# Hybrid attention layer on one core: scalings on ScalarE ordered behind the newest weight cast

## The chip, the core and the metric

The kernel runs on one core of a Trainium2 chip. The metric is the time of one execution on the device, in microseconds (us), median of the runs shown. Five engines work side by side, each through its own queue in order: TensorE (PE in the profile; its weight loads are PEld), VectorE (DVE), ScalarE (ACT), GpSimd (POOL) and SyncE (SP), which here only issues DMAs.

## The reference

One decoder layer over 256 tokens of width 2048, all in float32:

```python
mod = jax.nn.silu(c) @ w_ada + b_ada
shift, scale, gate = jnp.split(mod, 3, axis=-1)
h = _rms_norm(x, g_norm) * (1.0 + scale[:, None, :]) + shift[:, None, :]
proj = h @ w_in
qa, ka, va, za, q_idx, k_idx, w_idx, qb, kb, vb, zb = jnp.split(proj, COL_SPLITS, axis=-1)
qa = _rms_norm(qa.reshape(heads_a), q_norm_a)      # ka, qb, kb alike; k_idx over its 64 columns
ya = _dsa_attention(qa, ka, va, q_idx, k_idx, w_idx, _alibi_slopes(N_HEADS_A))
yb = _moba_attention(qb, kb, vb, _alibi_slopes(N_HEADS_B))
ya = ya.reshape(B, L, D_A) * jax.nn.silu(za)       # yb alike
y = jnp.concatenate([ya, yb], axis=-1) @ w_out
return x + gate[:, None, :] * y
```

`w_in` is 2048 by 9296, `w_out` 2048 by 2048, `w_ada` 2048 by 6144. Group a has eight heads of 128 columns that attend to 64 keys chosen by an indexer: sixteen small heads of 64 columns (`q_idx`), one shared key (`k_idx`), a relu, and a weighted sum give a score, and the 64 best keys stay. Group b has eight heads with plain causal attention, since 256 tokens are one block. What the change touches is the RMS norm of the queries, the keys and the indexer's key: each row of a head is multiplied by one over the root of its mean square.

## The kernel before

**Products.** Every weight is split in two parts before it is multiplied. ScalarE makes the high part (`cast_hi`, line 326, tile `wh`), VectorE the rest (`cast_lo`, line 336, tile `wl`), and TensorE makes three products of each block (lines 778 to 780: high by high, high by low, low by high). The unit is a step j: two blocks of 128 rows of weights by 512 columns, which is one cast `wh<j>`, one `wl<j>` and twelve matmuls (two blocks, two halves of the tokens, three products). `wh` and `wl` have four buffers each, and the weights as they land (`raw`) four of 8 KB a partition; SyncE issues a load as soon as a buffer of `raw` comes free. The casts are written two steps ahead of the matmuls (`LA = 2`, line 746).

**Order of the groups.** The columns of `w_in` are worked through in groups: the indexer's `i2`, `i0`, `i1`, then four quads of four heads, `b0`, `b1`, `a0`, `a1`, each as z, q, k, v; then the output product `mm_y`. A step's name in the profile says its group (`mm_h_vb` is a step of v of group b).

**Work between the steps.** Attention and norms are generators that `bg_q.step` advances after every step (line 788). Three of them matter here.
- `prep` (lines 504 to 518), for q and for k of each quad, as soon as its group is done: eight squares with sums on ScalarE (line 510), an add and a power -0.5 on GpSimd (`rsqrt`, lines 153 and 154), and eight scalings of 128 by 128 in place on ScalarE (line 517). The scalings need the power's result. `idx_k` does the same for the indexer's key with four scalings (line 456).
- `idx_pair` (lines 465 to 485), eight times, two index heads each: transposes `ptq` on TensorE (line 470), a copy `qi` out of PSUM on ScalarE (line 472), four small products `lg` on TensorE (lines 478 and 479), a relu `rl` for each head on ScalarE (line 481), and four additions on VectorE (line 483).
- `head` (lines 528 to 581): transposes of q and k, scores, exponentials, transposes (`pt`) and their copy `pT` on ScalarE (line 560), product with v (`pv`).

**What sets the order.** A scheduler builds one queue for each engine out of these written steps, and each engine takes its queue strictly from the front. An instruction that is not yet allowed to run holds up what is queued behind it on that engine. The helper `tc.add_manual_dep(..., NO_WAIT, ...)` (used by `in_order`, line 89) tells the scheduler that one instruction has to stand behind another of its engine; it adds no wait for a semaphore.

Of the kernel before, what the change touches and what calls it, by code (L numbers as in the profile page):

```python
# [10 lines left out]
AF = mybir.ActivationFunctionType  # L11
ALU = mybir.AluOpType

P = 128
# [4 lines left out]
HD = 128  # L19
# [29 lines left out]
NO_WAIT = mybir.DependencyInfo(mybir.DependencyClass.NoSync, mybir.DependencyReason.DATA)  # L49
# [3 lines left out]
def hybrid_block(ctx: ExitStack, tc: tile.TileContext, x, cols, w_ada_t, w_in, w_out, out):  # L53
    nc = tc.nc
# [11 lines left out]
    def late_tiles():  # L66
        if not late_pool:
            early.close()
            late_pool.append(ctx.enter_context(tc.tile_pool(name="late", bufs=2)))
        return late_pool[0]  # L70
# [12 lines left out]
    def ps_tile(tag, name):  # L83
        return psum.tile([P, 512], F32, tag=tag, bufs=1, name=name)

    last_on = {}

    @contextmanager
    def in_order():
# [61 lines left out]
    def rsqrt(dst, ssq, n):  # L151

        nc.gpsimd.tensor_scalar(dst, ssq, 1.0 / n, EPS, op0=ALU.mult, op1=ALU.add)
        nc.gpsimd.tensor_tensor(dst, dst, mhalf[:, :dst.shape[1]], op=ALU.pow)
# [46 lines left out]
    while turn:  # L201
# [22 lines left out]
        for k in range(seg0, end, 4):  # L224
            n = min(4, end - k)
# [76 lines left out]
    for li, ld in enumerate(loads):  # L302
        for m in ld.get("members", [ld] if ld["kind"] == "w" else []):
            n = len(m["kts"])
# [6 lines left out]
    def cast_hi(j):  # L311
        nonlocal next_load
        if j >= len(subs):
            return
        sb = subs[j]
        while next_load <= sb["li"]:
            issue(next_load + 6)
            if loads[next_load]["kind"] == "ada":
                gemv_todo.append(loads[next_load])
            next_load += 1  # L320
        flush_gemv()
        ld = sb["ld"]
        v = ld["v"][:, sb["o"]:sb["e"], :]
        n, w = v.shape[1], v.shape[2]
        hi = wsp.tile([P, 2, 512], F32R, tag="wh", name=f"wh{j}")
        nc.scalar.activation(hi[:, :n, :w], v, AF.Copy)  # L326
        sb["hi"] = hi

    def cast_lo(j):
# [11 lines left out]
    def flush_gemv():  # L341
        while gemv_todo:
            gemv(gemv_todo.pop(0))
# [94 lines left out]
    proj = {}  # L438
# [4 lines left out]
    sm = consts.tile([P, 64], F32, name="sm")  # L443

    def idx_k():
        for t in range(2):
            src = proj["i2", t]
            junk = work.tile([P, P], F32, name=f"junki{t}", tag="junk")
            nc.scalar.activation(junk[:, :64], src[:, 256:320], AF.Square, accum_out=sm[:, t:t + 1])
            nc.vector.tensor_scalar(w2[:, 16 * t:16 * t + 16], src[:, 320:336], 2.0 ** -5, None, op0=ALU.mult)  # L450
        rsqrt(sm[:, 2:4], sm[:, 0:2], 64)
        yield 0
        kk = late_tiles().tile([P, 384], F32, name="kk", tag="at", bufs=4)
        for t in range(2):
            for j in range(2):
                nc.scalar.activation(kk[:, t * P + j * 64:t * P + j * 64 + 64], proj["i2", t][:, 256:320],
                                     AF.Copy, scale=sm[:, 2 + t:3 + t])
        yield 0
        pt = ps_tile("pt", "ptk")
        for t in range(2):  # L460
            nc.tensor.transpose(pt[:, t * P:(t + 1) * P], kk[:, t * P:(t + 1) * P], ident)
        nc.scalar.activation(kiT, pt[:, :L], AF.Copy, scale=kidx_col)
        yield 0
# [40 lines left out]
    def prep(q, c):  # L504

        ssq = quad.setdefault((q, c), work.tile([P, 16], F32, name=f"ss{c}{q}", tag="ss", bufs=3))
        for t in range(2):
            for h in range(4):
                junk = work.tile([P, P], F32, name=f"j{c}{q}{t}{h}", tag="junk")
                nc.scalar.activation(junk, proj[c + q, t][:, h * HD:(h + 1) * HD], AF.Square,  # L510
                                     accum_out=ssq[:, 4 * t + h:4 * t + h + 1])
        rsqrt(ssq[:, 8:16], ssq[:, 0:8], HD)
        yield 2
        for t in range(2):
            for h in range(4):
                s = proj[c + q, t][:, h * HD:(h + 1) * HD]
                nc.scalar.activation(s, s, AF.Copy, scale=ssq[:, 8 + 4 * t + h:9 + 4 * t + h])
        yield 0

    def prep_z(q):  # L520
# [129 lines left out]
    with in_order():  # L650
        cast_hi(0)
        cast_lo(0)
        x_keep(0)
        start_mod()
        x_transpose(1)
# [5 lines left out]
    with in_order():  # L661
        for j in range(1, LA):
            cast_hi(j)
            cast_lo(j)
        x_keep(1)
# [45 lines left out]
    def group_done(g):  # L711

        if g[0] == "i":
            bg_q.done.add(g)
        if g == "i2":
            bg_q.add(chain(idx_k(), *[idx_pair(p) for p in (6, 7, 0, 1, 2, 3, 4, 5)], idx_top()), "top")
        if g[0] in "qk" and g[1] in "ab":
            bg_q.add(prep(g[1:], g[0]), "prep" + g)
        if g[0] == "k" and g[1] in "ab":
            pend.extend((g[1:], h) for h in range(4))  # L720
        if g[0] == "v":
            bg_q.done.add(g)
        if g[0] == "z":
            bg_q.add(prep_z(g[1:]), "prepz" + g[1:])

    total = len(subs)
    for j in range(total):
# [12 lines left out]
        if ld["kset"] == "y" and "xload" not in started:  # L740
            started.add("xload")
            for n in range(4):
                for t in range(2):
                    xr[n, t] = u_tile(f"xr{n}{t}")
                    nc.scalar.dma_start(xr[n, t], x[t * P:(t + 1) * P, n * 512:(n + 1) * 512])
        cast_hi(j + LA)
        cast_lo(j + LA)
        for c in ada_done:
# [73 lines left out]
```

## Time and profile before

| | us |
|---|---|
| median of 3 runs | 576.06 |
| lowest and highest run | 575.78, 577.69 |
| the profiled execution, its time | 576.41 |
| the profiled execution, its span on the core | 574.6 |
| PE busy | 553.2 (96%) |
| DVE busy | 443.5 (77%) |
| ACT busy | 319.5 (56%) |

The profile's times count from the span's start; the profiled execution's own time is 1.81 us more than its span. A page has the engines' busy time, the chain of work that ended last followed back from the last instruction, and the groups of instructions that cost most. Queries of the trace give instructions in order of time, with the idle time ahead of one and who ended it in brackets, and tables of busy time by stretch.

### The profile page before, as it was taken

What the parts mean: (1) busy time and instruction counts of PE and PEld (TensorE: products, weight loads), DVE (VectorE), ACT (ScalarE), POOL (GpSimd) and SP (SyncE); (2) the same over time, 40 slices, a digit from 0 to 9 for tenths busy, and PEclk for the clock granted to TensorE, in tenths of its full rate; (3) what the DMA queues carried; (4) which work ended last, traced back from release to release, by engine and by line L of the source; (5) the groups of instructions that cost most, each with busy time, mean ns of one, the idle gap of its engine ahead of it and who ended that gap; (6) DMA issues with size and microseconds to landing.
All of it is one profiled execution on the core that took longest, in us unless ns stands there. A gap on an engine that the chain in (4) does not pass through costs nothing.

```text
span 574.6 us, 7426 instructions
## 1 busy us (share of the span) xinstructions
PE 553.2 (96%) x2658; PEld 462.7 (81%) x2658; DVE 443.5 (77%) x681; ACT 319.5 (56%) x652; POOL 31.8 (6%) x56
## 2 busy tenths in 40 slices
PE   3889999999999999999899999999999999999996
PEld 2768888888889998887578888888888888887885
DVE  4887779898899888898789988697676575558452
ACT  4588564443444453577644577555775784554340
POOL 4100000000000000102100010200210110000000
PEclk9999999999999999999999999999999999999999
DMA  8999998997898988785864467787565458444701
GB/s 293 411 351 370 347 346 328 336 357 279 315 360 314 369 325 305 231 337 212 300 235 168 153 251 261 254 327 250 192 227 173 165 203 294 172 141 182 236 37 38
DMA packets 59670, 150.09 MB, mean 261 GB/s; under 512 B 3056, under 2 KB 9456, under 8 KB 53616
## 3 DMA queue, kind: packets, MB, share of 16 engines
q1 hardware_dynamic: 58480, 147.51, 71.0%
q10 hardware_dynamic: 1152, 2.10, 1.2%
q8 instruction: 21, 0.34, 0.2%
q14 instruction: 17, 0.14, 0.1%
HBM read 147.50 MB, written 2.10 MB: 260 GB/s over the span
## 4 chain that ended last, share of the span: by engine, by line
PE 88%; ACT 3%; DMA 2%; issue 2%; DVE 2%; POOL 2%; SPq 0%; DVEq 0%; ACTq 0%
PE mm_y_o L780 5%; PE mm_y_o L778 5%; PE mm_y_o L779 5%; PE mm_h_zb L778 3%; PE mm_h_zb L779 3%; PE mm_h_zb L780 3%; PE mm_h_i L780 3%; PE mm_h_i L779 3%; PE mm_h_i L778 3%; PE mm_h_qb L778 3%; PE mm_h_qb L779 3%; PE mm_h_qb L780 3%; PE mm_h_ka L779 3%; PE mm_h_qa L778 2%; PE mm_h_za L780 2%; PE mm_h_va L778 2%
## 5 line engine op out<-in xcount | busy, mean ns | idle before, releaser
L326 ACT ACTIVATE wh<-raw 128x1024 fp32r<-128x1024 f32 (+3 forms) x192 | 188.4, 991 | 148.0 <-PE mm_y_o L780 31.9
L336 DVE TENSOR_TENSOR wl<-raw,wh 128x1024 fp32r<-128x1024 f32 (+3 forms) x192 | 215.2, 1139 | 68.1 <-ACT wh L326 67.6
L293 DVE CUSTOM_DVE_ANT_0 raw<-raw,s_row 128x2048 f32<-128x2048 f32 (+1 forms) x49 | 110.0, 2245 | 4.9 <-DMA raw<-in_w_ada_t 4.8
L778 PE MATMUL mm_y_o<-wh,yT 128*128 128x512 f32 x128 | 51.6, 403 | 0.0
L779 PE MATMUL mm_y_o<-wl,yT 128*128 128x512 f32 x128 | 50.0, 391 | 0.0
L780 PE MATMUL mm_y_o<-wh,yT 128*128 128x512 f32 x128 | 49.9, 391 | 0.0
L778 PE MATMUL mm_h_i<-wh,hhi 128*128 128x384 f32 (+1 forms) x96 | 31.7, 330 | 0.0
L779 PE MATMUL mm_h_i<-wl,hhi 128*128 128x384 f32 (+1 forms) x96 | 31.5, 328 | 0.0
L780 PE MATMUL mm_h_i<-wh,hlo 128*128 128x384 f32 (+1 forms) x96 | 31.4, 328 | 0.0
L780 PEld LDWEIGHTS mm_y_o<-wh,yT 128*128 128x128 f32 x128 | 24.0, 188 | 5.2 <-DVE yT L579 0.2
L778 PEld LDWEIGHTS mm_y_o<-wh,yT 128*128 128x128 f32 x128 | 24.1, 188 | 4.7 <-ACT yT L578 0.2
L779 PEld LDWEIGHTS mm_y_o<-wl,yT 128*128 128x128 f32 x128 | 24.1, 188 | 4.6
L778 PE MATMUL mm_h_qa<-wh,hhi 128*128 128x512 f32 x64 | 25.7, 410 | 0.9 <-ACT wh L326 0.9
L778 PE MATMUL mm_h_zb<-wh,hhi 128*128 128x512 f32 x64 | 26.5, 413 | 0.0
L778 PE MATMUL mm_h_vb<-wh,hhi 128*128 128x512 f32 x64 | 26.1, 408 | 0.0
L779 PE MATMUL mm_h_za<-wl,hhi 128*128 128x512 f32 x64 | 25.1, 392 | 0.9 <-DVE wl L336 0.9
L778 PE MATMUL mm_h_kb<-wh,hhi 128*128 128x512 f32 x64 | 25.9, 407 | 0.0
L778 PE MATMUL mm_h_qb<-wh,hhi 128*128 128x512 f32 x64 | 25.6, 403 | 0.0
L779 PE MATMUL mm_h_zb<-wl,hhi 128*128 128x512 f32 x64 | 25.5, 398 | 0.0
L778 PE MATMUL mm_h_ka<-wh,hhi 128*128 128x512 f32 x64 | 25.5, 403 | 0.0
L778 PE MATMUL mm_h_va<-wh,hhi 128*128 128x512 f32 x64 | 25.4, 397 | 0.0
L780 PE MATMUL mm_h_zb<-wh,hlo 128*128 128x512 f32 x64 | 25.3, 398 | 0.0
(215 smaller groups left out, 1193.5 us busy)
## 6 DMA issues: line engine op xcount, KB each, us to landing
raw<-in_w_in SPq DMA_DIRECT2D x51, 1024.0 KB, 5.7
raw<-in_w_ada_t SPq DMA_DIRECT2D x47, 1024.0 KB, 6.3
raw<-in_w_out SPq DMA_DIRECT2D x16, 1024.0 KB, 5.3
raw<-in_w_in SPq DMA_DIRECT2D x17, 512.0 KB, 5.0
raw<-in_w_in SPq DMA_DIRECT2D x11, 768.0 KB, 5.3
x<-in_x SPq DMA_DIRECT2D x8, 256.0 KB, 7.3
xr<-in_x ACTq DMA_DIRECT2D x8, 256.0 KB, 8.4
raw<-in_w_in SPq DMA_DIRECT2D x3, 672.0 KB, 7.5
```

The costliest lines, as they stand in the source:

```text
L293: nc.vector.tensor_tensor_reduce(out=ld["v"], in0=ld["v"], in1=s_row[:, h0:h1], scale=1.0, scalar=0.0, op0=ALU.mult, op1=ALU.add, accum_ou ...
L326: nc.scalar.activation(hi[:, :n, :w], v, AF.Copy)
L336: nc.vector.tensor_tensor(lo[:, :n, :w], v, sb["hi"][:, :n, :w].bitcast(F32), op=ALU.subtract)
L778: nc.tensor.matmul(ps, a_hi, sb["hi"][:, i, :w], start=st, stop=False)
L779: nc.tensor.matmul(ps, a_hi, sb["lo"][:, i, :w], start=False, stop=False)
L780: nc.tensor.matmul(ps, a_lo, sb["hi"][:, i, :w], start=False, stop=en)
```

## The change

All scalings of `prep` and `idx_k` are put behind the newest high cast that has been written so far. Line numbers grow by 11 to 14 with it.

```diff
+    newest_cast = []
+
+    @contextmanager
+    def behind_cast():
+        traced = nc.cur_bb.bb.instructions
+        n = len(traced)
+        yield
+        for ins in traced[n:]:
+            if ins.engine == newest_cast[-1].engine:
+                tc.add_manual_dep(ins, newest_cast[-1].name, NO_WAIT, reason="behind_cast")
...
         nc.scalar.activation(hi[:, :n, :w], v, AF.Copy)
+        newest_cast.append(nc.cur_bb.bb.instructions[-1])
...
-        for t in range(2):
-            for j in range(2):
-                nc.scalar.activation(kk[:, t * P + j * 64:t * P + j * 64 + 64], proj["i2", t][:, 256:320],
-                                     AF.Copy, scale=sm[:, 2 + t:3 + t])
+        with behind_cast():
+            for t in range(2):
+                for j in range(2):
+                    nc.scalar.activation(kk[:, t * P + j * 64:t * P + j * 64 + 64], proj["i2", t][:, 256:320],
+                                         AF.Copy, scale=sm[:, 2 + t:3 + t])
...
-        for t in range(2):
-            for h in range(4):
-                s = proj[c + q, t][:, h * HD:(h + 1) * HD]
-                nc.scalar.activation(s, s, AF.Copy, scale=ssq[:, 8 + 4 * t + h:9 + 4 * t + h])
+        with behind_cast():
+            for t in range(2):
+                for h in range(4):
+                    s = proj[c + q, t][:, h * HD:(h + 1) * HD]
+                    nc.scalar.activation(s, s, AF.Copy, scale=ssq[:, 8 + 4 * t + h:9 + 4 * t + h])
```

There are 68 such scalings (four for the indexer's key, eight for q and eight for k of each of four quads). In the built programs the queues of PE, DVE, POOL and SP are the same before and after, and so is ACT's but for three scalings at two places.

The first place is ACT's queue while PE is on v of quad b0. `p_kb0_0` and `p_kb0_1` are the keys of quad b0 for either half of the tokens, scaled in place by `sskb0`; `wh106` to `wh108` are casts of weights, `qi3`, `rl6` and `rl7` belong to pair 3 of the index heads. Before:

```order
L510 ACTIVATE jkb013_2541,sskb0_2526<-p_kb0_1_784 128x128
L517 ACTIVATE p_kb0_0_782<-p_kb0_0_782,sskb0_2526 128x128 x2
L326 ACTIVATE wh106_2606<-raw98_2399 128x1024
L472 ACTIVATE qi3_2568<-ptq3_2565 128x256
L517 ACTIVATE p_kb0_0_782<-p_kb0_0_782,sskb0_2526 128x128 x2
L517 ACTIVATE p_kb0_1_784<-p_kb0_1_784,sskb0_2526 128x128 x4
L326 ACTIVATE wh107_2635<-raw98_2399 128x1024
L481 ACTIVATE rl6_2589<-lg6_2586 128x384
L481 ACTIVATE rl7_2596<-lg7_2593 128x384
L326 ACTIVATE wh108_2667<-raw99_2460 128x1024
```

After, on the same engine:

```order
L523 ACTIVATE jkb013_2541,sskb0_2526<-p_kb0_1_784 128x128
L337 ACTIVATE wh106_2606<-raw98_2399 128x1024
L485 ACTIVATE qi3_2568<-ptq3_2565 128x256
L531 ACTIVATE p_kb0_0_782<-p_kb0_0_782,sskb0_2526 128x128 x4
L531 ACTIVATE p_kb0_1_784<-p_kb0_1_784,sskb0_2526 128x128 x4
L337 ACTIVATE wh107_2635<-raw98_2399 128x1024
L494 ACTIVATE rl6_2589<-lg6_2586 128x384
L494 ACTIVATE rl7_2596<-lg7_2593 128x384
L337 ACTIVATE wh108_2667<-raw99_2460 128x1024
```

Two scalings have moved from ahead of `wh106` and `qi3` to behind them, and all eight now stand in a row.

The second place is ACT's queue while PE is on k of quad a1. `p_qa1_0` and `p_qa1_1` are the queries of quad a1, `pTa01` is the transposed probabilities of head 1 of quad a0. Before:

```order
L326 ACTIVATE wh157_4176<-raw138_3963 128x1024
L517 ACTIVATE p_qa1_0_503<-p_qa1_0_503,ssqa1_4118 128x128
L326 ACTIVATE wh158_4201<-raw138_3963 128x1024
L560 ACTIVATE pTa01_4169<-pta01_4165 128x384
L517 ACTIVATE p_qa1_0_503<-p_qa1_0_503,ssqa1_4118 128x128 x3
L517 ACTIVATE p_qa1_1_505<-p_qa1_1_505,ssqa1_4118 128x128 x4
L326 ACTIVATE wh159_4267<-raw139_3965 128x1024
```

After:

```order
L337 ACTIVATE wh157_4176<-raw138_3963 128x1024
L337 ACTIVATE wh158_4201<-raw138_3963 128x1024
L574 ACTIVATE pTa01_4169<-pta01_4165 128x384
L531 ACTIVATE p_qa1_0_503<-p_qa1_0_503,ssqa1_4118 128x128 x4
L531 ACTIVATE p_qa1_1_505<-p_qa1_1_505,ssqa1_4118 128x128 x4
L337 ACTIVATE wh159_4267<-raw139_3965 128x1024
```

One scaling has moved from ahead of `wh158` and `pTa01` to behind them.

PE's queue, which is the same in both, has this at the first place (the twelve matmuls of a step are shown by their first and last; the names are those of the program before):

```order
L470 MATMUL ptq3_2565<-ident_81,p_i1_1_658 128x128
L778 MATMUL mm_h4_vb0_0_2551<-wh103_2494,hhi6_1058 128x512
...
L780 MATMUL mm_h4_vb0_1_2552<-wh103_2494,hlo7_1066 128x512
L478 MATMUL lg6_2586<-kiT_182,qi3_2568 128x128
L479 MATMUL lg6_2586<-kiT_182,qi3_2568 128x256
L478 MATMUL lg7_2593<-kiT_182,qi3_2568 128x128
L479 MATMUL lg7_2593<-kiT_182,qi3_2568 128x256
L778 MATMUL mm_h4_vb0_0_2551<-wh104_2547,hhi8_1315 128x512
```

Nothing has moved on PE: the four `lg` products of pair 3 stand between the step of `wh103` and the step of `wh104`, and they take `qi3`.

## Rows read from the trace of the kernel before

**Rows 1.** The page: busy time by engine; the chain's shares by engine.

```profile
PE 553.2 (96%) x2658; PEld 462.7 (81%) x2658; DVE 443.5 (77%) x681; ACT 319.5 (56%) x652; POOL 31.8 (6%) x56
...
PE 88%; ACT 3%; DMA 2%; issue 2%; DVE 2%; POOL 2%; SPq 0%; DVEq 0%; ACTq 0%
```

**Rows 2.** Stretches: us, then PE, PEld, DVE, ACT, POOL busy; PEclk, DMA share, GB/s.

```profile
282.60:285.20 2.60, 0.07 (x1) 0.00 (x0) 0.26 (x1) 1.93 (x5) 0.64 (x1) 0.97 0.86 328
285.30:288.50 3.20, 3.20 (x12) 2.26 (x13) 3.20 (x4) 3.20 (x9) 0.00 (x0) 0.51 0.01 4
298.00:567.00 269.00, 269.00 (x1298) 223.76 (x1297) 192.71 (x363) 156.45 (x366) 15.01 (x12) 1.00 0.58 201
```

**Rows 3.** Chain of waits in order of time, 280 to 287: start, us, what.

```profile
281.50 1.75 POOL sskb L154
...
284.91 0.28 ACT qi L472
...
285.23 0.81 PE lg L478 x4
```

**Rows 4.** Timeline of PE, 282 to 298: start, us, instruction, idle before it and its releaser.

```profile
282.29 0.39 PE L780 MATMUL mm_h_vb<-wh,hlo 128*128 128x512 f32 x1
285.23 0.81 PE L478 MATMUL lg<-kiT,qi 64*128 64x128 f32 x4 [2.56 <-ACT qi L472]
...
290.42 0.38 PE L470 MATMUL ptq<-ident,p_i 128*128 128x128 f32 x2
...
293.19 0.39 PE L780 MATMUL mm_h_vb<-wh,hlo 128*128 128x512 f32 x1
293.50 0.50 PE L478 MATMUL lg<-kiT,qi 64*128 64x128 f32 x4
...
297.23 0.38 PE L470 MATMUL ptq<-ident,p_i 128*128 128x128 f32 x2
```

**Rows 5.** Timeline of ACT, 283 to 291, same columns.

```profile
283.27 0.69 ACT L517 ACTIVATE p_kb<-p_kb,sskb 128x128 f32<-128x128 f32 x2 [2.19 <-POOL sskb L154]
283.87 1.04 ACT L326 ACTIVATE wh<-raw 128x1024 fp32r<-128x1024 f32 x1
284.82 0.36 ACT L472 ACTIVATE qi<-ptq 128x256 f32<-128x256 f32 x1
285.08 1.85 ACT L517 ACTIVATE p_kb<-p_kb,sskb 128x128 f32<-128x128 f32 x6
286.84 1.04 ACT L326 ACTIVATE wh<-raw 128x1024 fp32r<-128x1024 f32 x1
287.79 0.84 ACT L481 ACTIVATE rl<-lg 128x384 f32<-128x384 f32 x2
290.62 1.06 ACT L326 ACTIVATE wh<-raw 128x1024 fp32r<-128x1024 f32 x1 [1.99 <-PE mm_h_vb L780]
```

**Rows 6.** Timeline of the DMA queue on SP, 268 to 283.

```profile
270.16 2.71 SPq L280 DMA_DIRECT2D raw<-in_w_in  x2
```

**Rows 7.** The page, DMA issues: count, KB each, median us from issue to landing.

```profile
raw<-in_w_in SPq DMA_DIRECT2D x51, 1024.0 KB, 5.7
```

**Rows 8.** Timeline of ACT, 454 to 457.

```profile
454.70 0.40 ACT L517 ACTIVATE p_qa<-p_qa,ssqa 128x128 f32<-128x128 f32 x1 [0.72 <-POOL ssqa L154]
455.01 1.04 ACT L326 ACTIVATE wh<-raw 128x1024 fp32r<-128x1024 f32 x1
455.95 0.47 ACT L560 ACTIVATE pTa<-pta 128x384 f32<-128x384 f32 x1
```

**Rows 9.** Timeline of PE, 460 to 461.

```profile
460.31 0.59 PE L567 MATMUL pva<-pTa,p_va 128*128 128x256 f32 x2
```

**Rows 10.** Timeline of POOL, 400 to 460.

```profile
405.61 3.74 POOL L154 TENSOR_TENSOR ssqa<-ssqa,mhalf 128x8 f32<-128x8 f32 x1
...
453.03 1.64 POOL L154 TENSOR_TENSOR ssqa<-ssqa,mhalf 128x8 f32<-128x8 f32 x1
```

**Rows 11.** Timeline of DVE at three places.

```profile
284.94 1.23 DVE L336 TENSOR_TENSOR wl<-raw,wh 128x1024 fp32r<-128x1024 f32 x1 [3.20 <-ACT wh L326]
...
405.56 2.29 DVE L293 CUSTOM_DVE_ANT_0 raw<-raw,s_row 128x2048 f32<-128x2048 f32 x1 [2.03 <-DMA raw<-in_w_ada_t]
...
454.01 1.23 DVE L336 TENSOR_TENSOR wl<-raw,wh 128x1024 fp32r<-128x1024 f32 x1 [1.18 <-ACT wh L326]
```

## The prediction

> **What bounds the kernel now.** Begin with the page: PE is busy 96% of the span, and 88% of the chain that ended last is PE's [rows 1]. So the question is not how much work ScalarE has (56%), but where PE stands still and whether the change is at such a place. The table by stretches then shows two things [rows 2]. From 298 to 567 PE is busy 269.00 of 269.00 us at a granted clock of 1.00 while the DMA engines are at 0.58: there is no wait on PE in which an earlier start could be lost. And between 282.60 and 285.20 PE is busy 0.07 of 2.60 us, followed by 3.2 us in which its clock is 0.51 of full speed. The chain of waits says what held PE there [rows 3]: GpSimd's power for the key norm (1.75 us), then ScalarE, whose `qi` copy releases the `lg` products. ScalarE's timeline gives the reason [rows 5]: it sat idle 2.19 us until the power was there, because two scalings of the keys stood at the front of its queue, and the cast `wh106` and the copy `qi3`, which need no power, stood behind them. PE's `lg` of pair 3 takes `qi3` and came at 285.23 after 2.56 us of idle time [rows 4].
>
> **The first place, step by step.** ScalarE was free at 283.27 - 2.19 = 281.08 [rows 5]. The two scalings now come later, so `wh106` can begin there, if its data and its buffer are there. The data (raw98) is the first of the pair of loads issued from 270.16 [rows 6]; at 5.7 us to landing [rows 7] it is there at about 276. Its buffer was last read by the step of `wh102`, which PE had behind it a whole step before 282.29. So both conditions are met with some 3 us to spare, estimated from these rows. The instruction behind the cast follows 284.82 - 283.87 = 0.95 us later, so `qi3` starts at 282.03 and, at 0.36 us, is done at 282.39. The hand-over to PE took 0.05 us before (284.82 + 0.36 = 285.18, `lg` at 285.23), which makes 282.44. PE itself can't be there before its last matmul of the step, at 282.29, and the usual 0.31 us to `lg` that the next round shows (293.19 to 293.50) [rows 4]: 282.60. So PE is now the later of the two, by 0.16 us, and the wait goes altogether.
>
> *Term 1, the wait*: 285.23 - 282.60 = 2.63 us.
>
> *Term 2, the clock*: from `lg` to the next `ptq` PE has four small products and twelve matmuls. In this round that took 290.42 - 285.23 = 5.19 us, in the next, the same work, 297.23 - 293.50 = 3.73 us [rows 4]. The difference is 1.46 us, and in just this stretch the granted clock was 0.51 (the 1.2 GHz level), against 1.00 (2.4 GHz) ahead of the wait and after it [rows 2]. The clock fell after PE had stood still, and nothing else in the stretch sets it apart. Without the wait I take the whole 1.46 back; the bounds are 0 and 1.46, and I take the upper one since the fall follows the idle time directly.
>
> **What the moved scalings delay.** They still start when the power is there, 283.27, as the squares that feed it have not moved. All eight now stand in a row: two took 0.60 (283.27 to 283.87), six 1.76 (285.08 to 286.84), so 2.36 us, and `wh107` starts at 285.63, which is 1.21 us earlier than before (286.84). With 0.95 for `wh107` and 0.84 for the two relus, `wh108` starts at 287.42 [rows 5]. Its buffer is free when the step of `wh104` ends, 282.60 + 3.73 = 286.33; its data, the second load of the pair (issued by 272.87), landed long before: between 285.30 and 288.50 the DMA engines were at 0.01, so what had been issued was all there [rows 2, 6]. `qi4` then starts at 288.37 and is done at 288.73. PE asks for it one round after `lg` of pair 3, that is at 282.60 + (293.50 - 285.23 - 1.46) = 289.41 [rows 4]. The margin is 289.41 - 288.73 - 0.05 = 0.63 us: small, but positive. From there ScalarE waits for PE to free a buffer, as it did before at 290.62 [rows 5], and the old pattern runs on, 4.09 us earlier. VectorE had been idle 3.20 us ahead of `wl106` [rows 11]; it gets that work earlier and has a step and more before PE needs it. The keys are used by transposes that stand after pair 4 on PE, so nobody waits for the scalings.
>
> **The second place.** ScalarE had 0.72 us of idle time ahead of the one scaling of qa1, and `wh158` and `pTa01` now start 1.03 us earlier (455.01 - 453.98) [rows 8]. The first to use `pTa01` is PE at 460.31 [rows 9], which is 460.31 - 456.42 = 3.89 us after the copy was done even before, and the step of `wh158` is later still. PE has no idle time there [rows 2]. The worth is 0; if I were wrong about that cover, at most the 1.03. The other 65 scalings stay where they were: they stood behind the newest cast already.
>
> **The sum.** 2.63 + 1.46 + 0 = 4.09 us less, against the profiled execution's 576.41: 572.32. That execution was 0.35 above the median, 576.06, so for the median I forecast 576.06 - 4.09 = 572.0 us, 0.71% less.
>
> **The rivals.**
>
> *The clock term does not come back.* If the slow stretch belongs to that point of the program and not to the wait, only term 1 is won: 576.06 - 2.63 = 573.4. Against it speaks that the clock is 1.00 all along until PE stands still. The Trainium skill, "TensorE: Matmul & The Clock Gate", section "What's actually happening", says that the clock's monitor runs free of the kernel, so that one and the same kernel shows slow stretches of different length from run to run. By that rule term 2 would lie between 0 and 1.46 by chance, and the time between 572.0 and 573.4. The three runs before speak for a steady one: without the slow stretch the profiled execution would have taken 576.41 - 1.46 = 574.95, and no run is below 575.78. Chance 0.07.
>
> *GpSimd's power comes later, and PE waits at pair 4 instead.* One power on GpSimd took 3.74 us, where a VectorE instruction (line 293) had begun 0.05 us ahead of it, and 1.64 us at 453.03, where VectorE's low cast began during the power, at 454.01, and neither was longer for it [rows 10, 11]. At the first place `wl106` now falls into the power's time: it can start at 282.1, the power starts at 281.50. That is the order of 453.03, so I take the power's time as it was. The Trainium skill, "SBUF — State Buffer", section "SBUF: two separate sides", says that GpSimd and a VectorE instruction with two inputs in SBUF lock each other out for a whole instruction, whoever began first. The slow power agrees with that; that the low cast at 454.01 kept its 1.23 us does not. Were the power as slow as the slowest row here (1.99 us more), the row of scalings would slip by as much, `qi4` would come 1.99 - 0.63 = 1.36 us late, and 2.73 us would be left: 573.3. Chance 0.05.
>
> *The gain is lost further on, or the change doesn't do what it says:* 576.1. What is won here could go into a later wait, if the next stretch were set by DMA or by VectorE. But from 298 on PE never waits [rows 2], and loads are issued when buffers come free, not at fixed times, so they move with PE. Or `wh106` finds its data or its buffer missing at 281.08, and `qi3` is as late as before. Only three of 68 instructions move, so without the first place there is nothing else to win. Chance 0.08.
>
> *Slower.* The place is the row of eight scalings, which now stands whole ahead of `wh107`, `wh108` and `qi4`. Each us by which it ends later than worked out, beyond 0.63, PE stands still at pair 4's `lg`, and if it stands about as long as at pair 3 the clock falls again for 1.46. It costs more than it wins when the wait there passes 2.63 us, a slip above 0.63 + 2.63 = 3.26; for 0.3% slower the slip has to be about 5.0. The slowest power explains 1.99. A load that lands late for `wh108` would have to add the rest, and the DMA engines had finished by then. With a slip of 5.0 the time is 576.06 + 1.7 = 577.8. Chance 0.04.
>
> **How the numbers follow.** Forecast 0.76, at 572.0; clock rival 0.07, at 573.4; late power 0.05, at up to 573.3; no gain 0.08, at 576.1; slower 0.04, at 577.8. The range goes down to 576.06 - 4.09 - 1.03 = 570.9, if the second place pays too, and up to 574.0, which takes in the first two rivals and some of the spread of the runs (575.78 to 577.69). It leaves out the last two, 0.12. A measurement of this kernel can tell about 0.3% (1.7 us) from no change: faster by more than that 0.76 + 0.07 + 0.05 = 0.88, within it 0.08, slower 0.04.
>
> **What would show it.** In the profile after: the cast ahead of `qi3` starts near 281.1 with no scaling ahead of it; `lg` of pair 3 near 282.6 without idle time named after `qi`; the granted clock 1.00 between 282 and 290; eight scalings from about 283.3; `lg` of pair 4 near 289.4 (before 293.50) without a wait; the cast of 290.62 near 287.4; and everything after it, the last matmul too, about 4.1 us earlier. The prediction is wrong in its first term if `lg` still comes near 285.2, in its second if the clock falls although PE did not stand still, and in its cover if PE is idle at 289.4.

## The result, and the profile after

The changed kernel takes 571.91 us (median of 9 runs, 570.66 to 573.70). The kernel before, run beside it, takes 574.41 us (median of 9, which are the three shown above and six more of 573.60 to 576.12). The ratio is 0.9943, with a 95% interval of 0.9923 to 0.9962: 0.57% less. So the forecast of 572.0 us was met as a time, but not as a gain: it was 4.09 us off 576.06, and 576.06 turned out to be a high value for the kernel before. The six later runs have a median of 574.0. Most of what follows is about that difference. One run of the experiments, the profiled one of `e5` at 801.77 us, had a mean granted clock of 0.66, is a slow one and enters no number below.

The profiled execution after took 571.33 us with a span of 569.6 us, against 576.41 and 574.6. The page's first row and its row of the chain by engine, to be read against [rows 1]:

```profile
PE 550.7 (97%) x2658; PEld 460.9 (81%) x2658; DVE 443.5 (78%) x681; ACT 319.2 (56%) x652; POOL 31.9 (6%) x56
...
PE 91%; ACT 3%; POOL 1%; DMA 1%; DVE 1%; issue 1%; SPq 0%; DVEq 0%; ACTq 0%
```

The chain has 91% on PE where it had 88%. PE's waits (engine, tile and line, waiting for what, then us in all, times, longest) have no `lg` waiting for `qi` any more; its largest are at the kernel's start:

```profile
PE ptx L389 <- POOL diag L376: 8.9, 2, 6.2
PE pts L144 <- DVE s_col L139: 3.4, 1, 3.4
PE mm_h_qa L792 <- ACT wh L337: 0.9, 1, 0.9
```

The stretches around the first place, and the long one behind it (columns as in [rows 2]):

```profile
280.00:284.00 4.00, 4.00 (x23) 2.83 (x22) 3.67 (x4) 3.03 (x9) 1.98 (x2) 1.00 0.86 289
284.00:290.00 6.00, 6.00 (x32) 4.50 (x31) 4.48 (x9) 5.02 (x11) 0.00 (x0) 1.00 0.77 274
...
295.00:564.00 269.00, 269.00 (x1296) 223.89 (x1295) 190.94 (x361) 155.57 (x364) 15.08 (x12) 1.00 0.58 198
```

PE is busy 4.00 of 4.00 us where it was busy 0.07 of 2.60, and its clock stays at 1.00 where it was 0.51 [rows 2]. From 295 to 564 it is busy without a gap, as it was from 298 to 567.

ScalarE's timeline there (start, us, instruction, idle time before it and its releaser) is the one that the change is about; it answers to [rows 5]:

```profile
279.89 1.06 ACT L337 ACTIVATE wh<-raw 128x1024 fp32r<-128x1024 f32 x1
280.84 0.37 ACT L485 ACTIVATE qi<-ptq 128x256 f32<-128x256 f32 x1
282.18 2.45 ACT L531 ACTIVATE p_kb<-p_kb,sskb 128x128 f32<-128x128 f32 x8 [0.97 <-POOL sskb L165]
284.54 1.04 ACT L337 ACTIVATE wh<-raw 128x1024 fp32r<-128x1024 f32 x1
285.49 0.84 ACT L494 ACTIVATE rl<-lg 128x384 f32<-128x384 f32 x2
286.23 1.05 ACT L337 ACTIVATE wh<-raw 128x1024 fp32r<-128x1024 f32 x1
287.18 0.37 ACT L485 ACTIVATE qi<-ptq 128x256 f32<-128x256 f32 x1
```

The cast `wh106` and the copy `qi3` now run while GpSimd still works on the power; eight scalings follow in a row. PE's timeline over the same round, answering to [rows 4]:

```profile
281.29 0.39 PE L794 MATMUL mm_h_vb<-wh,hlo 128*128 128x512 f32 x1
281.61 0.50 PE L491 MATMUL lg<-kiT,qi 64*128 64x128 f32 x4
...
285.34 0.38 PE L483 MATMUL ptq<-ident,p_i 128*128 128x128 f32 x2
...
288.42 0.50 PE L491 MATMUL lg<-kiT,qi 64*128 64x128 f32 x4
```

`lg` of pair 3 follows the last matmul of its step by 0.32 us, and `ptq` follows `lg` by 285.34 - 281.61 = 3.73 us, not 5.19. At pair 4 PE does not wait either.

**What of the 5.0 us between the two profiles is the change.** The last matmul of the step ahead of `lg` is at 281.29 after and at 282.29 before [rows 4]: 1.00 us is won ahead of the place where the change acts. It comes from the kernel's start. From 20 to 22 us, the kernel before and then the kernel after:

```profile
20.00:22.00 2.00, 2.00 (x6) 1.56 (x5) 2.00 (x4) 0.48 (x2) 0.00 (x0) 1.00 1.01 418
```

```profile
20.00:22.00 2.00, 2.00 (x15) 1.79 (x13) 2.00 (x4) 1.33 (x3) 0.00 (x0) 1.00 1.02 422
```

PE did 6 instructions in one and 15 in the other. In the profile before, the first projection's matmuls still followed one another at about 0.42 us there, and reached 0.23 us only by 23; in the profile after they were at 0.23 by 20. (In the profile before, the clock column reads 1.00 for the slow ones as well, so there it is not to be trusted and the pitch is. In the profile after, it reads 0.50 from 14 to 18 us, 0.52 from 18 to 20 and 1.00 behind that, as the pitch does.) At `ptq` of the first place the two kernels are 290.42 - 285.34 = 5.08 us apart, and at the last matmul of the program 569.85 - 564.76 = 5.09 us. So 5.08 - 1.00 = 4.08 us went at the first place in this pair, to 0.01 us what the sum said, and nothing was won or lost behind it.

### The profile page after: what moved, and what is told of

It reads as the page before. It is cut to its first block, busy times and chain, and to the rows that moved or that the text cites. A ratio compares the mean times of both kernels' runs of the same rounds, so it can differ in the third digit from the quotient of the medians.

```text
span 569.6 us, 7426 instructions
## 1 busy us (share of the span) xinstructions
PE 550.7 (97%) x2658; PEld 460.9 (81%) x2658; DVE 443.5 (78%) x681; ACT 319.2 (56%) x652; POOL 31.9 (6%) x56
## 4 chain that ended last, share of the span: by engine, by line
PE 91%; ACT 3%; POOL 1%; DMA 1%; DVE 1%; issue 1%; SPq 0%; DVEq 0%; ACTq 0%
PE mm_y_o L792 5%; PE mm_y_o L793 5%; PE mm_y_o L794 5%; PE mm_h_vb L792 3%; PE mm_h_zb L792 3%; PE mm_h_za L793 3%; PE mm_h_i L794 3%; PE mm_h_vb L794 3%; PE mm_h_i L792 3%; PE mm_h_zb L793 3%; PE mm_h_i L793 3%; PE mm_h_zb L794 3%; PE mm_h_za L794 3%; PE mm_h_qb L794 3%; PE mm_h_qb L793 3%; PE mm_h_qb L792 3%
## 5 line engine op out<-in xcount | busy, mean ns | idle before, releaser
L792 PE MATMUL mm_h_za<-wh,hhi 128*128 128x512 f32 x64 | 25.3, 402 | 0.4 <-ACT wh L337 0.4
L793 PE MATMUL mm_h_ka<-wl,hhi 128*128 128x512 f32 x64 | 25.1, 392 | 0.1
```

The source lines that it names most:

```text
L792: nc.tensor.matmul(ps, a_hi, sb["hi"][:, i, :w], start=st, stop=False)
L793: nc.tensor.matmul(ps, a_hi, sb["lo"][:, i, :w], start=False, stop=False)
```

## The experiments

Two theories stood against each other. By the first, that of the prediction, each execution of the kernel before loses 2.63 us of waiting and then 1.46 us to a lower clock. By the second the wait is always there, but the clock falls after it in some executions only, so that a part of the 4.09 us is won only there. Two side questions were the second place, and the rival of a late power. In all of them "before" is the kernel before, run on the same chip beside the experiment, and of its times the medians and means are of 17 to 32 runs.

### Which place brings the gain

The change at one place alone: `e2` keeps it for the keys of quad b0, `e3` for the queries of quad a1.

```diff
-    def behind_cast():
+    def behind_cast(on=True):
...
-            if ins.engine == newest_cast[-1].engine:
+            if on and ins.engine == newest_cast[-1].engine:
...
-        with behind_cast():
+        with behind_cast(False):
...
-        with behind_cast():
+        with behind_cast((q, c) == ("b0", "k")):
```

The last line of `e3` has `("a1", "q")` instead; the line with `False` is that of the indexer keys, in both.

> Only the eight scalings of the keys of quad b0 are put behind the newest cast; ScalarE's queue differs from before at the first place alone. My theory (the whole gain is at the first place): the same as the changed kernel, 571.9, ratio to before about 0.9945, no wait at lg of pair 3. Rival (the second place pays too): about 1.0 us slower than the changed kernel, 572.9.

> Only the eight scalings of the queries of quad a1 are put behind the newest cast; ScalarE's queue differs from before at the second place alone. My theory: the same as before, ratio 1.000, with the wait at lg of pair 3 as before, and the cast and pT there about 1.0 us earlier with nobody on PE who takes it. Rival: about 1.0 us less, ratio 0.998.

`e2`: 571.62 us (median of 9) beside 575.72 of before (median of 32), ratio 0.9934 (0.9913 to 0.9955); the means are 571.76 and 575.62, which is 3.86 us. `e3`: 575.75 us (median of 12), ratio 0.9996 (0.9975 to 1.0018). The first place brings all of the gain, the second nothing that can be measured. `e3`'s profile still has the wait, and behind it the low clock (stretches, columns as in [rows 2]):

```profile
282.40:284.80 2.40, 0.01 (x1) 0.00 (x0) 0.24 (x1) 1.91 (x5) 0.46 (x1) 1.00 0.88 341
284.90:288.10 3.20, 3.20 (x12) 2.26 (x13) 3.20 (x4) 3.20 (x9) 0.00 (x0) 0.50 0.00 0
```

### Does the clock fall in every execution of the kernel before

`e1` and `e11` are the kernel before, with no edit: twelve runs, and a single profiled one.

> The kernel before, unchanged, timed against itself. Theory 1 (the wait of 2.63 us and the slow clock of 1.46 us belong to every execution): this profile has the wait ahead of lg of pair 3 and a granted clock near 0.5 right after it, all runs show a mean clock of 0.997 or less, and the spread of the runs (573.6 to 577.7 so far) comes from elsewhere. Theory 2 (the fall of the clock comes in some executions only): some runs have a mean clock of 1.000 and are about 1.5 us shorter than the others, and then the gain of the change is 2.6 us against those and 4.1 against the others. Either way the ratio to itself is 1.000.

> The kernel before, once more for one profile. Theory 2: if the time is 575.6 or above, the granted clock is near 0.5 after the wait ahead of lg of pair 3, and longer than 3.3 us if the time is above 577; if it is below 575, the clock stays at 1.00. In both, lg of pair 3 comes about 2.6 us late.

`e1`: 574.65 us (median of 12, 573.77 to 577.16), ratio 0.9993 (0.9973 to 1.0013), profiled at 574.10. `e11`: 574.13 us. In `e1`'s profile the wait is as it was, and the clock does not fall. Its timeline of PE, and its stretches:

```profile
283.82 0.50 PE L478 MATMUL lg<-kiT,qi 64*128 64x128 f32 x4 [2.38 <-ACT qi L472]
...
287.56 0.38 PE L470 MATMUL ptq<-ident,p_i 128*128 128x128 f32 x2
```

```profile
280.00:284.00 4.00, 1.62 (x9) 1.03 (x9) 0.80 (x2) 2.14 (x6) 1.75 (x1) 1.00 0.86 315
284.00:290.00 6.00, 6.00 (x32) 4.70 (x32) 6.00 (x9) 4.54 (x11) 0.00 (x0) 1.00 0.32 92
```

PE is busy 1.62 of 4.00 us, and from `lg` to `ptq` it takes 287.56 - 283.82 = 3.74 us. `e11` shows the same, with `lg` idle for 2.43 us before it and a clock of 1.00 behind:

```profile
284.43 0.50 PE L478 MATMUL lg<-kiT,qi 64*128 64x128 f32 x4 [2.43 <-ACT qi L472]
...
288.14 0.38 PE L470 MATMUL ptq<-ident,p_i 128*128 128x128 f32 x2
```

So of three profiled executions of the kernel before one paid the clock term and two did not, with 2.56, 2.38 and 2.43 us of idle time ahead. The first theory falls here: the term is not part of every execution.

`e4` takes the idle time away and leaves the wait: seven matmuls of 512 columns on PE, ahead of `lg` of pair 3, into a PSUM bank that nothing reads. `lg` still needs `qi3`, which comes no earlier.

```diff
+            if h == 6:
+                fill = ps_tile("pt", "fill")
+                for _ in range(7):
+                    nc.tensor.matmul(fill, hhi[6][:, :P], step_hi[0][:, 0, :], start=True, stop=True)
...
+    step_hi = [None]
...
+        step_hi[0] = sb["hi"]
```

`step_hi[0]` is the high cast of the step that was worked through last.

> The kernel before, with seven matmuls of 512 columns put on PE ahead of lg of pair 3, into a bank of PSUM that nobody reads; they fill about 1.6 of the 2.6 us in which PE stood still, and move nothing else in any queue. Theory 1 (the clock falls because PE stands still): the clock stays at 1.00 or falls for less, lg still comes near 285.2, and the kernel is up to 1.46 us faster than before (ratio 0.9975). Theory 2 (the fall comes in some executions only): between 0 and 1.46 us, by how many executions of before have the fall. Rival (the fall belongs to that point of the program): clock near 0.5 after lg all the same, ratio 1.000.

`e4`: 574.72 us (median of 12), ratio 0.9984 (0.9968 to 1.0000). None of its runs is above 575.72, where 16 of the 32 runs of before are. Its timeline of PE shows the filler, 0.67 us of idle time that is left, and 287.69 - 283.94 = 3.75 us to `ptq`:

```profile
281.52 1.75 PE L481 MATMUL fill<-wh,hhi 128*128 128x512 f32 x7
283.94 0.50 PE L482 MATMUL lg<-kiT,qi 64*128 64x128 f32 x4 [0.67 <-ACT qi L472]
...
287.69 0.38 PE L470 MATMUL ptq<-ident,p_i 128*128 128x128 f32 x2
```

`e2` and `e4` ran on the same chip beside the same runs of before, and so divide the gain. By the means, before to `e4` is 575.62 - 574.69 = 0.93 us, an estimate of what the falls of the clock cost on average; `e4` to `e2` is 574.69 - 571.76 = 2.93 us, which is the wait alone. The sum had 1.46 and 2.63. With the interval of `e4` the first of these lies between 0.0 and 1.8 us, so its size is rough; that the filler takes away the upper half of the spread is plain.

`e5` makes the wait longer instead: the power of the keys of quad b0 is made twice, with the same values. `e10` is the same kernel, profiled once more.

```diff
         rsqrt(ssq[:, 8:16], ssq[:, 0:8], HD)
+        if (q, c) == ("b0", "k"):
+            rsqrt(ssq[:, 8:16], ssq[:, 0:8], HD)
```

> The kernel before, with GpSimd's add and power for the keys of quad b0 made a second time (same values, some 1.9 us more on GpSimd). The scheduler then also puts qi3 ahead of wh106, still behind two scalings, which takes 0.95 us off, so PE should stand still about 3.5 us ahead of lg of pair 3 instead of 2.6. Theory 2 as it stands now (PE's clock falls in some executions only, and in more of them the longer PE stands still): nearly all runs show a mean clock of 0.997 or below 0.99, none or few are without the fall, and the median is about 0.95 us of wait plus about 1 us of clock above before (ratio 1.003 to 1.004). Theory 1 (the fall comes every time with a wait of 2.6 us already, and the spread of before comes from elsewhere): 0.95 us more and the same spread (ratio 1.0017).

> The kernel before with the power made twice, once more for one profile, since its first one was disturbed. The add made a second time took 2.22 us, not 0.24, in the changed kernel, since VectorE's line 293 ran; here VectorE has nothing to do meanwhile, so 1.9 us more on GpSimd, some 3.5 us of wait ahead of lg of pair 3, and a granted clock near 0.5 right after it.

`e5`: 579.28 us (median of 9), ratio 1.0060 (1.0034 to 1.0085), and none of the nine runs is below 576.20. `e10`: 577.62 us. `e10`'s timeline of PE, and its stretches:

```profile
286.37 0.81 PE L478 MATMUL lg<-kiT,qi 64*128 64x128 f32 x4 [4.93 <-ACT qi L472]
...
291.64 0.38 PE L470 MATMUL ptq<-ident,p_i 128*128 128x128 f32 x2
```

```profile
281.40:286.30 4.90, 0.04 (x1) 0.00 (x0) 2.70 (x4) 0.95 (x4) 3.66 (x4) 1.00 0.68 237
286.40:289.60 3.20, 3.20 (x12) 2.26 (x13) 1.23 (x1) 3.20 (x8) 0.00 (x0) 0.50 0.65 202
```

With 4.93 us of idle time the clock falls, and `ptq` comes 5.27 us after `lg`. The idle time is 1.4 us longer than the 3.5 that was expected. VectorE shows why: its line 293 stands ahead of the copy `p_kb`, which the squares on ScalarE read, and it waited for a load. `e10`, then before:

```profile
274.06 2.29 DVE L293 CUSTOM_DVE_ANT_0 raw<-raw,s_row 128x2048 f32<-128x2048 f32 x1 [1.53 <-DMA raw<-in_w_ada_t]
```

```profile
273.99 2.29 DVE L293 CUSTOM_DVE_ANT_0 raw<-raw,s_row 128x2048 f32<-128x2048 f32 x1 [0.19 <-DMA raw<-in_w_ada_t]
```

In `e1` and `e11` it did not wait at all. So the wait at pair 3 also grows when this load comes late. `e5` lost 578.71 - 575.59 = 3.1 us by the means; how much of that is the wait and how much the clock is not shown, since `e10`, this kernel's profile, has the late load. This is weaker than `e4` also because the scheduler moved two more things in this kernel: `qi3` ahead of `wh106` on ScalarE, and the low cast `wl106` behind line 293 on VectorE.

### The late power

`e6` is the changed kernel with the same power made twice, so that the eight scalings come late on purpose. `e9` is the same kernel, profiled once more.

```diff
         rsqrt(ssq[:, 8:16], ssq[:, 0:8], HD)
+        if (q, c) == ("b0", "k"):
+            rsqrt(ssq[:, 8:16], ssq[:, 0:8], HD)
         yield 2
         with behind_cast():
```

> The changed kernel, with GpSimd's add and power for the keys of quad b0 made a second time; no other queue differs from the changed kernel. My theory (the row of eight scalings has a margin of 0.63 us before pair 4 waits for it; 0.87 in the trace of the changed kernel): the row starts some 1.9 us later, PE waits about 1.0 to 1.3 us at lg of pair 4, named after qi, its clock stays at 1.00, and the time is about 573 (ratio to before 0.996 to 0.997). Rival (the order keeps PE free of the power altogether): as the changed kernel, 571.8.

> The changed kernel with the power made twice, once more for one profile: its first profile had the wait of 3.1 us without a fall of the clock, at 574.37. If this one is near 576 or above, theory 2 wants a stretch of the granted clock near 0.5 right after the wait ahead of lg of pair 4; if near 573 to 575, none.

`e6`: 576.76 us (median of 12, 573.03 to 578.84), ratio 1.0018 (0.9995 to 1.0042): the whole gain is gone. Ten of its runs are above the 574.37 of its profile, and no profile shows what they lose beyond the wait. `e9`: 572.70 us. The two profiles part at one GpSimd instruction, the second add. `e6`'s timeline of GpSimd, and the VectorE instruction beside it:

```profile
280.19 1.75 POOL L165 TENSOR_TENSOR sskb<-sskb,mhalf 128x8 f32<-128x8 f32 x1
282.02 2.22 POOL L164 TENSOR_SCALAR sskb<-sskb 128x8 f32<-128x8 f32 x1
284.33 1.64 POOL L165 TENSOR_TENSOR sskb<-sskb,mhalf 128x8 f32<-128x8 f32 x1
```

```profile
281.91 2.29 DVE L304 CUSTOM_DVE_ANT_0 raw<-raw,s_row 128x2048 f32<-128x2048 f32 x1
```

and the same of `e9`:

```profile
282.36 0.20 POOL L164 TENSOR_SCALAR sskb<-sskb 128x8 f32<-128x8 f32 x1
282.64 1.64 POOL L165 TENSOR_TENSOR sskb<-sskb,mhalf 128x8 f32<-128x8 f32 x1
```

```profile
283.40 2.29 DVE L304 CUSTOM_DVE_ANT_0 raw<-raw,s_row 128x2048 f32<-128x2048 f32 x1 [1.06 <-DMA raw<-in_w_ada_t]
```

The add of `e6` started 0.11 us after VectorE's line 304 and took 2.22 us, to the end of that instruction; the add of `e9` was ahead of it and took 0.20. The power ended at 285.97 in one and at 284.28 in the other, and PE's wait at pair 4 followed. PE's timeline, `e6`, then `e9`, with the `ptq` ahead of it:

```profile
285.16 0.38 PE L483 MATMUL ptq<-ident,p_i 128*128 128x128 f32 x2
...
291.41 0.50 PE L491 MATMUL lg<-kiT,qi 64*128 64x128 f32 x4 [3.12 <-ACT qi L485]
```

```profile
285.52 0.38 PE L483 MATMUL ptq<-ident,p_i 128*128 128x128 f32 x2
...
289.74 0.50 PE L491 MATMUL lg<-kiT,qi 64*128 64x128 f32 x4 [1.09 <-ACT qi L485]
```

So the rival's mechanism is real: a scaling row that slips moves the wait to pair 4. In neither profile did the clock fall behind it, so 3.12 us of idle time too can leave the clock at 1.00 (`e6`'s stretch behind the wait, columns as in [rows 2]):

```profile
291.40:296.00 4.60, 4.59 (x25) 3.58 (x26) 4.60 (x9) 2.41 (x4) 0.00 (x0) 1.00 0.73 245
```

`e8` fills that wait, as `e4` filled the other: `e6` with ten matmuls of 512 columns ahead of `lg` of pair 4, and an ordering of VectorE's queue that keeps it as it was.

```diff
+            if h == 8:
+                fill = ps_tile("pt", "fill")
+                for _ in range(10):
+                    nc.tensor.matmul(fill, hhi[6][:, :P], step_hi[0][:, 0, :], start=True, stop=True)
...
```

The lines for that ordering, for `step_hi` and for the second power are left out here.

> The changed kernel with GpSimd's power made twice, and ten matmuls of 512 columns on PE ahead of lg of pair 4, into a bank of PSUM that nobody reads, so that PE works through 2.3 of the 3.1 us in which it stood still there; no other queue differs from the kernel with the power made twice. Without the fill that kernel ran 573.0 to 578.8, median 576.76. Theory 2 (what goes beyond the wait is the clock, which falls in some executions when PE stands still): lg of pair 4 comes as late as before, but the runs gather at the lower end, 573 to 575, median about 574.5, ratio to before 0.997 to 0.998, and the clock is 1.00 after the wait. Rival (the upper half of the runs comes from something else that waits, a load or VectorE): the same spread up to 578.8.

`e8`: 574.89 us (median of 12, eleven of them at or below 575.61), ratio 1.0000 (0.9980 to 1.0020). Of `e6`'s twelve runs seven are above 575.61. In its profile the power is as late as in `e6` (an add of 2.23 us at 282.92), and what is left of the wait, in its table of waits, is

```profile
PE lg L501 <- ACT qi L491: 0.9, 1, 0.9
```

By the means `e6` is 0.88 us above its before (576.47 and 575.59) and `e8` 0.12 below its own (575.00 and 575.12): 1.0 us between the two. The intervals of the two ratios overlap, and how often the add fell behind line 304 in the runs of either is not known, so these runs alone do not show that the idle time costs it; the direction agrees with `e4`.

### The clock at the start

`e7` is the changed kernel with fillers on PE ahead of the first x transposes, 12 and then 6 matmuls of 128 columns, to have the clock up earlier in each execution.

```diff
+    def warm(n):
+        fill = ps_tile("pv", f"warm{n}")
+        for _ in range(n):
+            nc.tensor.matmul(fill[:, :P], ident, ident, start=True, stop=True)
+
...
+            if k2 == 0:
+                warm(12 if t == 0 else 6)
```

> The changed kernel, with 12 and 6 matmuls of 128 columns on PE ahead of the first transposes of x, while PE waits there for GpSimd, into a bank of PSUM that nobody reads. In every profile so far PE's first matmuls of the projection, at 19 to 22 us, run at the slow pitch of 0.43 us, and executions differ by about 1 us there. If PE's work at the start is what that spread comes from, the pitch is 0.23 us from the first of them on, and the kernel gains up to 1 us on the changed one (571.0, ratio to before 0.992) with a smaller spread. Rival (the start is set by VectorE and DMA anyway): as the changed kernel, since PE waits for casts at 32 and 39 us all the same.

`e7`: 573.80 us (median of 12), ratio 0.9961 (0.9940 to 0.9982): no better than the change alone (0.9934 and 0.9943), if anything worse. The second projection step did start earlier, at 20.95 us where the profile after has 21.93, but it was lost again. Its stretches show where:

```profile
30.00:32.00 2.00, 0.47 (x5) 0.28 (x3) 1.61 (x2) 0.02 (x1) 0.00 (x0) 1.00 1.10 420
...
34.00:36.00 2.00, 2.00 (x6) 1.51 (x6) 1.26 (x3) 1.37 (x3) 0.00 (x0) 0.50 1.05 393
```

PE ran dry from 30 to 32 us, and two us later its clock was 0.50. The profile after has PE busy 1.33 of 2.00 in the first of these stretches, and a clock of 1.00 in the second. PE waited 2.19 us for ScalarE's casts there (0.38 in the profile after), and the casts for a load. ScalarE in `e7`, then after:

```profile
31.98 2.20 ACT L337 ACTIVATE wh<-raw 128x512 fp32r<-128x512 f32 x4 [2.72 <-DMA raw<-in_w_in]
```

```profile
31.15 2.19 ACT L337 ACTIVATE wh<-raw 128x512 fp32r<-128x512 f32 x4 [0.91 <-DMA raw<-in_w_in]
```

PE came 1 us earlier, but the load did not: in this pair it let ScalarE begin 0.83 us later. So what was won ahead of it was lost in waiting for it, as the rival in the expectation had it, and the clock fell besides. Why the load was later is not settled; the order of PE's first instructions also moved a little with the fillers. (The expectation reads the slow pitch up to 22 us in every profile; in the profile after it ended by 20.)

## Why the prediction was right, and where it was not

**Term 1, the wait (2.63 us): right.** `lg` moved from 2.94 us behind the last matmul of its step (285.23 - 282.29) to 0.32 us (281.61 - 281.29): 2.62 us. The steps held too. The profile after runs 1.00 us ahead at that point; with that added back, `wh106` starts at 280.89 (281.08 was worked out), `qi3` at 281.84 (282.03), `lg` at 282.61 (282.60), the scalings at 283.18 (283.27), and they take 2.45 us (2.36). The wait, 2.38 to 2.56 us of idle time, is in all four profiles in which the first place is as before and PE has no filler (before, `e1`, `e3`, `e11`), and it is in none of those with the first place changed. `e4` to `e2` prices it at 2.9 us, which is rough with the spread of the runs.

**Term 2, the clock (1.46 us): the mechanism was right, its size as an average was not.** Where the clock falls it costs what [rows 2, 4] showed, in this round it falls only behind the wait, and the change takes it away. But it does not fall each time: of the executions profiled, yes in the first and in `e3`, no in `e1` and `e11`. The step that failed was the argument for a steady term, "no run is below 575.78". It rested on three runs. An execution without the slow stretch was to take 574.95, and `e1` at 574.10 and `e11` at 574.13 are such executions. The rival by the Trainium skill, "TensorE: Matmul & The Clock Gate", section "What's actually happening" (the monitor of the clock runs free of the kernel, and how many slow matmuls a kernel starts with varies from run to run), was the better account of this term. The traces agree with it, here in the middle of the kernel: three executions of one program with 2.56, 2.38 and 2.43 us of idle time, 5.19, 3.74 and 3.71 us from `lg` to `ptq`. What decides in which execution it falls no run here shows.

**The sum.** The mean clock that is listed with each run fits the picture. In the 32 runs of before that `e1` to `e4` share, the 12 at 0.997, the value of the two profiles in which the clock fell, take 576.24 on average (575.65 to 576.92); the 9 at 0.989 and 0.991, the values of the two in which it did not, take 574.59. That reading is no proof for a single run, since other stretches lower the mean too, above all the start. Five more of the 32 are at 577.22 to 578.84, above both groups. None of these was profiled, so what they lose is open: a longer fall of the clock, or a longer wait as in `e10`. The gain is then 2.6 us in some executions, 4.1 in others, and more against those five. By the medians it was 574.41 - 571.91 = 2.50 us in one comparison and 575.72 - 571.62 = 4.10 in the other, since the median of before falls now into one group and now into the other; by the means it was 2.88 and 3.86. Half a clock term would make 2.63 + 0.73 = 3.36. All are above 0.3%, so the sign and the range held. The time of 572.0 held because the profile before had the fall, and the three runs beside it were by their times (575.78 and above) of the same kind, so that the whole 4.09 comes off. That the three were of one kind was luck: with a median of the other kind, as the six later runs gave it, the same sum would have come out about 2 us too low.

**The cover of the moved scalings: right.** `qi4` is done at 287.18 + 0.37 = 287.55 and PE asks at 288.42: with the hand-over of 0.05 us the margin is 0.82, where 0.63 was worked out. `e6` and `e9` test it. Their second power ends at 285.97 and 284.28, where the one of the profile after ends at 282.15; their PE is 0.18 us ahead and 0.18 us behind at `ptq` (285.16 and 285.52, against 285.34). The scalings slip by 4.00 and 1.95 us then, which should leave 4.00 - 0.82 = 3.18 and 1.95 - 0.82 = 1.13 us of waiting at pair 4. It was 3.12 and 1.09.

**The rival of a late power: a real mechanism that did not occur.** In the profile after the power takes 1.75 us as before. VectorE's low cast began inside it and kept its 1.23 us, and the long line 304 came just as it ended:

```profile
280.40 1.75 POOL L165 TENSOR_TENSOR sskb<-sskb,mhalf 128x8 f32<-128x8 f32 x1
```

```profile
280.98 1.23 DVE L348 TENSOR_TENSOR wl<-raw,wh 128x1024 fp32r<-128x1024 f32 x1 [0.33 <-ACT wh L337]
...
282.12 2.29 DVE L304 CUSTOM_DVE_ANT_0 raw<-raw,s_row 128x2048 f32<-128x2048 f32 x1
```

The forecast took [rows 10, 11] over the rule of the Trainium skill, "SBUF — State Buffer", section "SBUF: two separate sides", by which the one that begins first locks the other out whole, and for this order that was right: the cast was not delayed. For the other order, a VectorE instruction that began first, `e6`'s add of 2.22 us agrees with the rule. Line 304 began 1.72 us after the power did and stands behind the low cast on VectorE's queue, so in this order it can come ahead of the power only if the low cast does too. Had it begun ahead, as it did with `e6`'s second add, PE would have stood at pair 4.

**The second place: right, nothing.** `e3` measures no difference. The copy `pTa01` came 6.03 us earlier, 5.08 of it with everything else and 0.95 by the change (1.03 was worked out), and PE takes it at 455.24, 4.8 us after it was done:

```profile
449.92 0.48 ACT L574 ACTIVATE pTa<-pta 128x384 f32<-128x384 f32 x1
```

**No gain, and slower:** neither came. PE still has no idle time in the 269 us behind the place, so nothing could take the gain back.

## What to carry to other kernels

On an engine that runs its queue in strict order, work that waits for a slow neighbour belongs behind the work that another engine is about to ask for; price the move by the wait that ends on the bounding engine, and follow the moved row to the next such request, whose margin (0.82 us here) is the new risk. A fall of the clock that one profile shows behind a wait is not a cost of each execution: look at several before it goes into a sum in full, and say which kind the time to be beaten belongs to. To tell a wait's price from that of the clock behind it, fill the wait with work that nothing reads, as `e4` does.

## What the runs showed of the hardware that was not expected

- Behind one and the same wait, TensorE's clock fell to 0.50 or 0.51 of full speed (the 1.2 GHz level) in some executions and stayed at 1.00 (2.4 GHz) in others: it fell in two and stayed in two that were profiled with 2.4 to 2.6 us of idle time, stayed with 3.12 us in one (`e6`), and fell with 4.93 us in one (`e10`). Where it fell, 3.73 us of matmuls took 5.2 to 5.3.
- At the start of the kernel the matmuls came to the fast pitch of 0.23 us by 20 us in the profile after and only by 23 in the one before, with the same instructions in front of them. That alone is 1.0 us between two profiles, and it can be taken for an effect of the change by someone who compares the spans alone.
- A GpSimd add of 128x8 that takes 0.20 to 0.24 us took 2.22 us when VectorE's line 304 had begun 0.11 us before it, while a VectorE cast that began inside a GpSimd power kept its 1.23 us, and line 304, begun inside the second power of `e9`, its 2.29. Who begins first decided who waited only in the one direction.
